# The FFN's last output tile made for 128 tokens at a time, with the update and the mixer's first product in halves

## The chip, the cores and the metric

The kernel runs on one core of one Trainium2 chip. The metric is the device time of one execution in microseconds (us); the median of the runs is compared. Engines are named as the profile names them: PE (TensorE, the matmuls), PEld (its weight loads), DVE (VectorE), ACT (ScalarE), POOL (GpSimd), SP (SyncE, which issues most transfers).

## What is computed

An encoder trunk of four layers on 256 tokens of width 1024, in float32. Each layer is a half-step feed-forward branch (FFN, SwiGLU, hidden width 2816), a token mixer, and a second FFN. Layers 0 and 3 use mixer A (chunked attention), layer 1 mixer B (a gated MLP with a mixing matrix over tokens), layer 2 mixer C (differential attention).

```python
def rms_norm(x, g):
    y = x * rsqrt(mean(x * x, axis=-1) + EPS)
    return y * g

def swiglu(h, w_in, w_out):
    gate, up = split(h @ w_in, 2, axis=-1)
    return (silu(gate) * up) @ w_out

for i in range(DEPTH):
    g = norm_g[i]
    x = x + 0.5 * rms_norm(swiglu(rms_norm(x, g[0]), ff1_w_in[i], ff1_w_out[i]), g[1])
    h = rms_norm(x, g[2])
    x = x + rms_norm(mixer(h), g[3])
    x = x + 0.5 * rms_norm(swiglu(rms_norm(x, g[4]), ff2_w_in[i], ff2_w_out[i]), g[5])
```

The norm after a branch needs the branch's whole output: the factor of a token is known only when all 1024 features of it are there. That is the junction this case is about.

## The kernel before

**Layout.** Activations are kept transposed: 128 features on the partitions, tokens along the free dimension, so `xr` (the residual stream) is 8 tiles of 128 features by 256 tokens. A weight is split on the chip into a high part in fp32r and the rest (`w_hi`, `w_lo`: a cast on ACT, L126, and a subtraction on DVE, L129), and so are the activations (`h` and `l`, stored side by side as `x[:, k, 0, :]` and `x[:, k, 1, :]`). A product is three passes: high by high, high by low, low by high.

**Weights.** `Stream` (`W`) loads raw pieces through SP into three raw buffers of two pieces each, splits them into eight slots, and hands them out with `peek` and `done`; `done(n, most)` frees n pieces and lets at most `most` new ones be split; `hold` stops splitting and `resume` starts it again. PE's, DVE's and ACT's instructions run in the order in which the program writes them.

**Forms of product.** `product2` (L175 to L186) makes one matmul of 512 columns (the weight's high part with the activations' high and low parts side by side) and one of 256 (the weight's low part). The two halves of the result are then added: ACT copies the second half (`share`), DVE adds. `product` (L164 to L171) makes three matmuls of 256 columns straight into one result, with no addition afterwards. `Wide` (L686 on) takes activations of 128 tokens as the weights and streams 512 columns of the weight matrix, for the mixers' first product; its result has tokens on the partitions, in two banks of PSUM, one for each half of the tokens.

**The FFN's end.** `ffn` (L557) makes eight output tiles d. Tiles 0 to 6 use `product2`; `Branch.joined` adds the halves, squares the tile, adds the square into `acc`, and scales the tile by the gain into `yg`. Tile 7 uses `product` (L168). Then `tile_done` sums the squares over the features with `column_sums` (matmuls with a column of ones, L243), `finish` makes the factor of each token (`inv_sqrt`: a square root on ACT, L251, a reciprocal on DVE, L253), `spread2` copies it to all partitions by matmuls (L258), and an `Update` is returned: x gains `yg` times the spread factor.

**Made ahead.** While this chain runs, PE has work that needs no factor: `Ahead`. Before a mixer (`wide=True`) it makes, for the first 128 tokens and k = 2 and 3, the mixer's first product of the old x and of `yg` apart (12 matmuls of 512 columns, L455); the second is scaled by the factor and added later (`scale`, `join`). Between a mixer and the second FFN, and between layers, it does the like for the FFN's first product (L457).

**The next stage's start.** `Normed` updates x in the order of `PARTS` (multiply on DVE, add on DVE, high part on ACT, low part on DVE), sums the squares of the new x, and PE follows through `Wide` in the order `JOIN` as the tiles get ready. After the last FFN there is no next stage: eight DVE passes over two tiles each (a multiply and an add, four times) and four transfers write the output.

Of the kernel before, what the change touches and what calls it, by code (L numbers as in the profile page):

```python
# [16 lines left out]
P = 128  # L17
# [33 lines left out]
YLATE = {4: (0, 1), 5: (2, 3)}  # L51
JOIN = _order([k for a, b in PARTS for k in range(a, b)])
# [4 lines left out]
def encoder_trunk_kernel(  # L57
# [207 lines left out]

    class Normed:


        def __init__(self, update, gain):
# [5 lines left out]
            if update is None:  # L275
                self.begin(gain)
            else:
# [39 lines left out]
        def high(self, gain, a, b):  # L317
            for k in range(a, b):
                nc.scalar.activation(self.h[:, k, :], xr[:, k, :], AF.Copy, scale=gain[:, k:k + 1])  # L319
# [12 lines left out]
        def low(self, gain, a, b):  # L332
            for k in range(a, b):
                nc.vector.scalar_tensor_tensor(
                    self.l[:, k, :], xr[:, k, :], gain[:, k:k + 1], self.h[:, k, :].bitcast(F32),
# [24 lines left out]
    class Branch:  # L360
# [37 lines left out]

        def finish(self):
# [7 lines left out]
    class Ahead:  # L407


        def __init__(self, gain, wide=False, late=False):  # L410
            self.gain, self.wide, self.late = gain, wide, late
            self.ks = (2, 3) if wide else (0, 1, 2, 3)
            self.x, self.y, self.todo = {}, {}, []
# [23 lines left out]
        def begin(self):  # L437

            self.ps, self.share = pair(), bank()
            for o, xs in ((self.ps[:, 0, :], self.x), (self.share, self.y)):  # L440
                for k in self.ks:
                    if self.wide:
                        wh, wl = [part.rearrange("p (k c) -> p k c", k=2)[:, k % 2, :] for part in W.peek(k // 2)]
                    else:
                        wh, wl = [part[:, k, :] for part in blocks(W.peek())]
# [5 lines left out]
        def __call__(self, n):  # L451
            while self.todo and n > 0:
                o, w_, x, first, last = self.todo.pop(0)
                if self.wide:
                    nc.tensor.matmul(o, x[:, 0:P], w_, start=first, stop=last, skip_group_check=True)  # L455
                else:
                    nc.tensor.matmul(o[:, 0:S], w_, x, start=first, stop=last, skip_group_check=True)  # L457
                n -= 2 if self.wide else 1

        def scale(self, update):  # L460

            if self.wide:
                self.fy = tmp.tile([P, 512], F32, tag="hf", bufs=3, name="fy")
                nc.scalar.activation(self.fy, self.share, AF.Copy, scale=update.f[:, 0:1])
            else:
                self.fy = tmp.tile([P, S], F32, tag="gs", name="fy")
                nc.scalar.copy(self.fy, self.share[:, 0:S])
                nc.vector.tensor_tensor(self.fy, self.fy, update.fb, op=ALU.mult)

        def join(self):  # L470
            o = self.ps[:, 0, :] if self.wide else self.ps[:, 0, 0:S]
            nc.vector.tensor_tensor(o, o, self.fy, op=ALU.add)

    class Update:


        def __init__(self, yg, f, fb, ahead):
            self.yg, self.f, self.fb, self.ahead, self.t = yg, f, fb, ahead, {}

        def multiply(self, a, b):  # L480
            t = tmp.tile([P, 2, S], F32, tag="upd", name="upd")[:, 0:b - a, :]
            nc.vector.tensor_tensor(
                t, self.yg[:, a:b, :], self.fb.unsqueeze(1).broadcast_to([P, b - a, S]), op=ALU.mult
# [3 lines left out]
        def add(self, a, b):  # L487
            nc.vector.tensor_tensor(xr[:, a:b, :], xr[:, a:b, :], self.t.pop(a), op=ALU.add)  # L488
# [68 lines left out]
    def ffn(l, which, update, ahead):  # L557
# [58 lines left out]
        nc.scalar.preload_act_table(AF.Sqrt)  # L616
        br = Branch(g_sb[:, l, 4 * which + 1, :], n, ahead)
        b = 0
        for d in range(KD):
# [22 lines left out]
            if ahead:  # L642
                ahead.x_parts(d)
        return br.finish()
# [41 lines left out]
    class Wide:  # L686


        def __init__(self, n):
            self.n, self.q, self.ahead = n, 0, n.ahead  # L690

        def block(self, piece, kk, low):
            wh, wl = [part.rearrange("p (k c) -> p k c", k=2)[:, kk % 2, :] for part in piece]
            for xs, ws in ((self.n.l, wh),) if low else ((self.n.h, wh), (self.n.h, wl)):
                for t in range(2):
                    if t == 0 and self.ahead and kk in self.ahead.ks:
                        continue
# [574 lines left out]
```

## Time and profile before

| | |
|---|---|
| median of 3 runs | 1940.93 us (1940.19 to 1941.04) |
| the profiled execution's own time | 1942.05 us |
| its span in the profile | 1940.3 us |
| mean granted TensorE clock | 0.999 |
| weight load (PEld) busy | 90% of the span |
| HBM traffic | 347.31 MB read, 1.05 MB written |

How to read the views: a row of the page or of the groups gives line, engine, operation, what is written and read, partitions x elements, count, then busy microseconds, mean nanoseconds of one, idle time ahead of it and what ended it. Successive matmuls overlap in the records, so the mean duration of one is not the distance from one to the next; that distance comes from the chain, which gives start, length and count. A row of the timeline begins with start and length in microseconds.

### The profile page before, as it was taken

To read this page: it belongs to the slowest core of one execution; us is meant where nothing else is said; L and a number is where in the kernel's file an instruction comes from. 1 tells how busy PE (TensorE), PEld (TensorE's weight loads), DVE (VectorE), ACT (ScalarE), POOL (GpSimd) and SP (SyncE) were. 2 spreads that over 40 slices of the span, in tenths; PEclk is the share of its full clock that TensorE was granted. 3 is DMA by queue.
4 is the path that set the end of the run, shared out by engine and by line. 5 is a ranking of instruction groups with operands and counts; after the bars stand their busy time and mean duration, and the time that the engine had idled before them with its cause. 6 is when DMAs were issued, how large, how long until landed. Compare 5 with 4: busy or idle time off the path is not lost.

```text
span 1940.3 us, 29924 instructions
## 1 busy us (share of the span) xinstructions
PE 1928.2 (99%) x12354; PEld 1741.4 (90%) x12354; DVE 1388.3 (72%) x1883; ACT 1168.6 (60%) x1797; POOL 5.2 (0%) x19
## 2 busy tenths in 40 slices
PE   9999999999999999999999999999999999999998
PEld 8888999888988899888988899988898889998887
DVE  6775767876777587876676668786768766868763
ACT  6655557656555566656565665775656555666552
POOL 0000000000000000000000000000000000000000
PEclk9999999999999999999999999999999999999999
DMA  7555524555455544655455544365445554535551
GB/s 257 203 193 197 194 109 152 218 194 195 154 207 183 203 168 151 229 186 198 147 213 188 188 158 169 109 214 196 177 163 205 194 197 168 196 115 186 200 201 44
DMA packets 50393, 350.30 MB, mean 181 GB/s; under 512 B 5712, under 2 KB 5968, under 8 KB 9040
## 3 DMA queue, kind: packets, MB, share of 16 engines
q1 hardware_dynamic: 48096, 341.86, 48.7%
q10 hardware_dynamic: 2160, 6.52, 0.9%
q8 instruction: 97, 1.59, 0.3%
q14 instruction: 40, 0.33, 0.0%
HBM read 347.31 MB, written 1.05 MB: 180 GB/s over the span
## 4 chain that ended last, share of the span: by engine, by line
PE 98%; DVE 1%; DMA 0%; ACT 0%; SPq 0%; issue 0%; DVEq 0%
PE pp_t L182 68%; PE pp_t L535 8%; PE pp_t L168 7%; PE pp_t L698 4%; PE pp_t L516 4%; PE pp_t L657 2%; PE pp_t L738 1%; PE pst_t L770 1%; PE pp_t L457 1%; PE pst_t L243 1%; PE pst_t L457 1%; PE pp_t L892 0%; PE pst_t L258 0%; DVE rbc L352 0%; PE pp_t L455 0%; DMA w_raw<-in_w 0%
## 5 line engine op out<-in xcount | busy, mean ns | idle before, releaser
L129 DVE TENSOR_TENSOR w_lo<-w_raw,w_hi 128x1024 fp32r<-128x1024 f32 (+1 forms) x649 | 775.7, 1218 | 61.8 <-ACT w_hi L126 61.6
L126 ACT CAST w_hi<-w_raw 128x1024 fp32r<-128x1024 f32 (+1 forms) x649 | 668.8, 1045 | 161.5 <-PE pp_t L182 130.1
L182 PE MATMUL pp_t<-xp,w_hi 128*128 128x512 f32 x2560 | 612.9, 391 | 0.0
L182 PEld LDWEIGHTS pp_t<-xp,w_hi 128*128 128x128 f32 x2560 | 470.2, 188 | 90.8
L182 PEld LDWEIGHTS pp_t<-xp,w_lo 128*128 128x128 f32 x2560 | 329.2, 191 | 16.1 <-DVE w_lo L129 3.4
L182 PE MATMUL pp_t<-xp,w_lo 128*128 128x256 f32 x2560 | 335.1, 283 | 2.6 <-DVE w_lo L129 2.6
L604 DVE TENSOR_TENSOR gu<-pp_t,share 128x512 f32<-128x512 f32 x160 | 110.4, 690 | 201.6 <-ACT share L603 201.6
L603 ACT COPY share<-pp_t 128x512 f32<-128x512 f32 x160 | 93.5, 584 | 145.9 <-PE pp_t L182 145.3
L182 PE MATMUL pp_t<-h,w_hi 128*128 128x512 f32 x672 | 169.0, 391 | 0.0
L576 ACT ACTIVATE gs<-gs 128x512 f32<-128x512 f32 x88 | 55.7, 633 | 145.5 <-DVE gs L575 145.5
L182 PE MATMUL pp_t<-l,w_hi 128*128 128x512 f32 x560 | 142.6, 391 | 0.0
L182 PEld LDWEIGHTS pp_t<-h,w_hi 128*128 128x128 f32 x672 | 122.1, 189 | 22.6
L535 PE MATMUL pp_t<-xp,w_hi 128*128 128x256 f32 x832 | 125.0, 289 | 1.1 <-ACT w_hi L126 0.7
L182 PEld LDWEIGHTS pp_t<-l,w_hi 128*128 128x128 f32 x560 | 102.6, 188 | 21.1 <-DVE l L585 1.6
L535 PEld LDWEIGHTS pp_t<-xp,w_hi 128*128 128x128 f32 x832 | 112.2, 194 | 3.5 <-ACT w_hi L126 1.2
L373 DVE TENSOR_TENSOR yg<-pp_t,share 128x256 f32<-128x256 f32 x56 | 23.8, 425 | 108.8 <-ACT share L372 108.8
L182 PEld LDWEIGHTS pp_t<-h,w_lo 128*128 128x128 f32 x672 | 91.1, 191 | 5.0
L182 PE MATMUL pp_t<-h,w_lo 128*128 128x256 f32 x672 | 95.2, 282 | 0.0
L182 PE MATMUL pp_t<-l,w_lo 128*128 128x256 f32 x560 | 80.6, 283 | 0.0
L319 ACT ACTIVATE xp<-xr,g_sb 128x256 fp32r<-128x256 f32 x96 | 44.8, 504 | 55.9 <-DVE xr L488 54.0
L182 PEld LDWEIGHTS pp_t<-l,w_lo 128*128 128x128 f32 x560 | 75.4, 191 | 2.8
L535 PE MATMUL pp_t<-xp,w_lo 128*128 128x256 f32 x416 | 74.3, 285 | 0.0
(201 smaller groups left out, 2254.3 us busy)
## 6 DMA issues: line engine op xcount, KB each, us to landing
w_raw<-in_w SPq DMA_DIRECT2D x322, 1024.0 KB, 4.8
l<-in_a_bias ACTq DMA_DIRECT2D x8, 512.0 KB, 7.5
w_raw<-in_w SPq DMA_DIRECT2D x3, 512.0 KB, 8.6
out_y<-xr SPq DMA_DIRECT2D x4, 256.0 KB, 2.1
xr<-in_x_t SPq DMA_DIRECT2D x2, 384.0 KB, 6.8
w_raw<-in_w SPq DMA_DIRECT2D x2, 256.0 KB, 5.0
l<-in_b_ws ACTq DMA_DIRECT2D x1, 512.0 KB, 5.8
l<-in_b_ln_g ACTq DMA_DIRECT2D x1, 512.0 KB, 7.3
```

The costliest lines, as they stand in the source:

```text
L126: nc.scalar.copy(hi[:, cols], raw[:, cols])
L129: nc.vector.tensor_tensor(lo[:, cols], raw[:, cols], hi[:, cols].bitcast(F32), op=ALU.subtract)
L168: nc.tensor.matmul(o, w_[:, at + i, :], x(k)[:, low, :], start=(start and i == 0 and m == 0), stop=(stop and k == ks[-1] and m == 2),)
L182: nc.tensor.matmul(o[:, 0:S] if low else o, (wl if low else wh)[:, at + i, :], x(k)[:, 0, :] if low else x(k), start=(start and i == 0 and ...
L319: nc.scalar.activation(self.h[:, k, :], xr[:, k, :], AF.Copy, scale=gain[:, k:k + 1])
L457: nc.tensor.matmul(o[:, 0:S], w_, x, start=first, stop=last, skip_group_check=True)
L516: nc.tensor.matmul(o, part[:, k, :], n.x[:, k, int(low), :], start=((k, low) == JOIN[0] and i == 2 and part is ws[i][0]), stop=((k, low) = ...
L535: nc.tensor.matmul(o, part[:, k, :], n.x[:, k, low, :], start=(at == 0), stop=(at == 3 * KD - 1))
L576: nc.scalar.activation(gs, gs, AF.Silu)
L603: nc.scalar.copy(share, ps[:, :, S:2 * S])
L604: nc.vector.tensor_tensor(at.t[:, e], ps[:, :, 0:S], share, op=ALU.add)
L698: nc.tensor.matmul(self.ps[:, t, :], xs[:, kk, t * P:(t + 1) * P], ws, start=((kk, low) == self.order[0] and ws is wh and not (t == 0 and ...
```

## The change

It affects five of the eight FFNs: the first of each layer, which stands ahead of a mixer, and the very last (`halved = which == 0 or not ahead`).

- Tile 7 of these FFNs is made by `last_halves`: for each half t of the tokens, 22 matmuls of 256 columns (high and low parts of 128 tokens side by side) and 22 of 128 columns. The sum, the squares, the factor and its spread are made for each half. Those of half 0 run while PE works on half 1. The three weight pieces of the tile are given back only after both halves, behind `hold`.
- `Normed.halves` takes the place of the update in `PARTS` order. It updates 128 tokens of the tiles in the order of `HALF_PARTS`, lets `Wide` make the first half of the mixer's product (24 matmuls of 512 columns), with the steps of half 1's factor laid in between, and then updates the other 128 tokens. `Wide.first` makes the second half.
- `Ahead(wide=True)` is removed with all its cases, so nothing is made ahead of a mixer. The `Ahead` of the other junctions stays.
- At the end of the kernel the output's half 0 is updated and written first, in two transfers, then half 1.

```diff
+HALF_PARTS = ((0, 1), (1, 2), (2, 4), (4, 6), (6, 8))
...
+        def halves(self, up, gain):
+            self.wide = Wide(self)
+            br = up.br
+            for a, b in HALF_PARTS:
+                if a == 6:
+                    br.half_sum(1)
+                up.multiply(a, b, 0)
+                up.add(a, b, 0)
+                self.high(gain, a, b, 0)
+            br.half_square(1, lambda: self.low(gain, 0, 4, 0))
+            self.wide.half(0, 0, 17)
+            br.half_factor(1, lambda: self.low(gain, 4, 6, 0))
+            self.low(gain, 6, KD, 0)
+            self.wide.half(0, 17, 20)
+            br.half_spread(1)
+            self.wide.half(0, 20, 24)
+            for a, b in HALF_PARTS:
+                up.multiply(a, b, 1)
+                up.add(a, b, 1)
+                self.high(gain, a, b, 1)
+            self.low(gain, 0, KD, 1)
+            W.resume(1)
+            W.settle()
+            for a in (0, 2, 4, 6):
+                self.square(a)
+            self.total()
+            W.pump(1)
...
+        def last_halves(self, blocks):
+            self.o = pair()
+            self.fs, self.fbs = {}, {}
+            for t in range(2):
+                todo = []
+                cols = tokens(t)
+                for run in blocks:
+                    turn[0] = not turn[0]
+                    for low in (False, True) if turn[0] else (True, False):
+                        todo += [(low, wl if low else wh, x) for wh, wl, x in run]
+                for i, (low, w_, x) in enumerate(todo):
+                    nc.tensor.matmul(
+                        self.o[:, t, 0:P] if low else self.o[:, t, 0:2 * P], w_, x[:, 0, cols] if low else x[:, :, cols],
+                        start=(i == 0), stop=(i == len(todo) - 1), skip_group_check=True,
+                    )
+                    if t == 1 and i == 19:
+                        self.half_factor(0)
+                    if t == 1 and i == 29:
+                        self.half_spread(0)
+                if t == 0:
+                    self.half_sum(0)
+                    self.half_square(0)
+            return Update(self.yg, None, None, None, self)
+
+        def half_sum(self, t):
+            share = tmp.tile([P, 2, S], F32, tag="upd", name="share")[:, 0, 0:P]
+            nc.scalar.copy(share, self.o[:, t, P:2 * P])
+            nc.vector.tensor_tensor(self.yg[:, KD - 1, tokens(t)], self.o[:, t, 0:P], share, op=ALU.add)
+
+        def half_square(self, t, then=lambda: None):
+            y, acc = self.yg[:, KD - 1, tokens(t)], self.acc[:, tokens(t)]
+            sq = tmp.tile([P, S], F32, tag="sq1", name="sq1")[:, 0:P]
+            nc.scalar.activation(sq, y, AF.Square)
+            nc.scalar.activation(y, y, AF.Copy, scale=self.gain[:, KD - 1:KD])
+            then()
+            nc.vector.tensor_tensor(acc, acc, sq, op=ALU.add)
+
+        def half_factor(self, t, then=lambda: None):
+            ss = bank()[:, 0:1]
+            nc.tensor.matmul(ss, self.acc[:, tokens(t)], ones[:, 0:1], start=True, stop=True)
+            then()
+            self.fs[t] = inv_sqrt(ss, eps2_t if self.n else eps_t, 1, 1.0 / D)
+
+        def half_spread(self, t):
+            self.fbs[t] = bank()[:, 0:P]
+            spread(self.fs[t], self.fbs[t])
...
+            up = br.last_halves(runs)
+            W.hold()
+            W.done(i)
+            return up
...
+        def half(self, t, a, b):
+            for i in range(a, b):
+                k, low, m = self.todo[i]
+                nc.tensor.matmul(
+                    self.ps[:, t, :], self.n.x[:, k, low, tokens(t)],
+                    W.peek(k // 2)[m].rearrange("p (k c) -> p k c", k=2)[:, k % 2, :],
+                    start=(i == 0), stop=(i == len(self.todo) - 1), skip_group_check=True,
+                )
+
+        def first(self):
+            self.half(1, 0, len(self.todo))
+            W.done(4, 3)
...
-        update = ffn(l, 0, update, Ahead(g_sb[:, l, 2, :], True))
+        update = ffn(l, 0, update, None)
...
+    fill = Warm()
+    fill(6)
+    update.multiply(0, 4, 0)
+    result(0, 4, 0)
+    update.multiply(4, KD, 0)
+    br.half_sum(1)
+    br.half_square(1, lambda: result(4, KD, 0))
+    br.half_factor(1)
+    fill(4)
+    br.half_spread(1)
+    for a, b in ((0, 4), (4, KD)):
+        update.multiply(a, b, 1)
+        result(a, b, 1)
```

`result(a, b, half)` adds the update to x for these tiles and tokens and issues the transfer of them. The order `todo` of `Wide` is: for each k the high activations with the weight's high and low part, then for each k the low activations with the high part.

More of the change, by code (lines that the diff above doesn't have):

```diff
@@ L276, in __init__ @@
                 self.begin(gain)
+            elif update.halved:
+                self.halves(update, gain)
             else:
@@ L453, in __call__ @@
                 o, w_, x, first, last = self.todo.pop(0)
[L454 to L458, printed above, removed]
-        def scale(self, update):
[L462 to L468, printed above, removed]
+                nc.tensor.matmul(o[:, 0:S], w_, x, start=first, stop=last, skip_group_check=True)
@@ L470, in join, with __init__ @@
+                n -= 1
+        def scale(self, update):
+            self.fy = tmp.tile([P, S], F32, tag="gs", name="fy")
+            nc.scalar.copy(self.fy, self.share[:, 0:S])
+            nc.vector.tensor_tensor(self.fy, self.fy, update.fb, op=ALU.mult)
         def join(self):
-            o = self.ps[:, 0, :] if self.wide else self.ps[:, 0, 0:S]
+            o = self.ps[:, 0, 0:S]
             nc.vector.tensor_tensor(o, o, self.fy, op=ALU.add)
     class Update:
-        def __init__(self, yg, f, fb, ahead):
+        def __init__(self, yg, f, fb, ahead, halved=None):
@@ L616, in ffn @@
         nc.scalar.preload_act_table(AF.Sqrt)
+        halved = which == 0 or not ahead
         br = Branch(g_sb[:, l, 4 * which + 1, :], n, ahead)
         b = 0
-        for d in range(KD):
+        for d in range(KD - 1 if halved else KD):
             apart = d < KD - 1
@@ L643, in ffn @@
                 ahead.x_parts(d)
+        if halved:
+            runs, k, i = [], 0, 0
+            while k < NJ:
+                wh, wl = blocks(W.peek(i))
+                n_ = min(KD - b, NJ - k)
+                runs.append([(wh[:, b + m, :], wl[:, b + m, :], hidden(k + m)[:, 0]) for m in range(n_)])
+                k, b, i = k + n_, 0, i + 1
+            up = br.last_halves(runs)
+            W.hold()
+            W.done(i)
+            return up
         return br.finish()
@@ L695, in block @@
                 for t in range(2):
-                    if t == 0 and self.ahead and kk in self.ahead.ks:
-                        continue
                     nc.tensor.matmul(
                         self.ps[:, t, :], xs[:, kk, t * P:(t + 1) * P], ws,
-                        start=((kk, low) == self.order[0] and ws is wh and not (t == 0 and self.ahead)),
+                        start=((kk, low) == self.order[0] and ws is wh),
                         stop=((kk, low) == self.order[-1]), skip_group_check=True,
@@ L710, in run @@
                     soon()
-                if low and kk % 2 and not self.ahead:
+                if low and kk % 2:
                     if kk == KD - 1:
@@ L716, in run @@
                     self.q = (kk + 1) // 2 % 4
-            if self.ahead:
-                self.ahead.join()
-                W.done(4, most)
-            self.ahead = None
     BLOCKS = ((0, 0), (1, 1), (1, 0))
@@ L773, in attention @@
     def attention(n, softmax, transposes, v_done, mix, prepare=lambda: None, soon=lambda: None):
-        wide = Wide(n)
-        wide.run()
+        wide = n.wide
+        wide.first()
         ps_v = wide.ps
@@ L948, in v_done @@
                 nc.vector.bn_stats(st[:, t, c, :], v[:, t, c * 512:(c + 1) * 512])
-        wide = Wide(n)
-        wide.run()
+        wide = n.wide
+        wide.first()
         for k in range(KD):
```

56 lines of the change are left out of this document (31 added, 25 removed).

## The prediction

> **What bounds the kernel now.** I read the page first (busy shares, then the chain that ended last), then the chain in order of time around the first place the change touches, then the same chain at the other places, then the groups by shape for durations, and last the vector engines' groups. PE is TensorE, DVE VectorE, ACT ScalarE.
>
> ```profile
> span 1940.3 us, 29924 instructions
> PE 1928.2 (99%) x12354; PEld 1741.4 (90%) x12354; DVE 1388.3 (72%) x1883; ACT 1168.6 (60%) x1797; POOL 5.2 (0%) x19
> PE 98%; DVE 1%; DMA 0%; ACT 0%; SPq 0%; issue 0%; DVEq 0%
> 188.52 7.92 PE pp_t L168 x66
> 196.44 0.34 PE pst_t L243 x4
> ...
> 200.70 9.63 PE pp_t L698 x42
> 210.33 2.87 PE pp_t L535 x24
> 213.21 0.34 PE pst_t L243 x4
> 213.55 2.98 PE pp_t L535 x24
> 216.52 0.44 PE pst_t L258 x4
> ```
>
> PE carries 98% of the chain: a microsecond on PE's own list is a microsecond of time, one on DVE or ACT counts only where PE stands still for it. The chain rows are columns of start, length, what. They show the first site (layer 0, FFN 1 into mixer A): the last output tile is 66 matmuls in 7.92 us, so **120 ns** for one of 256 columns; then 4.26 us of sums, spreads and the 12 matmuls made ahead; then 42 matmuls of 512 columns in 9.63 us, **229 ns** each. From the tile's start to the mixer's next product: 210.33 - 188.52 = **21.81 us**. The other three sites, and the tail:
>
> ```profile
> 678.71 7.92 PE pp_t L168 x66
> 690.83 13.24 PE pp_t L698 x58
> 1130.69 7.92 PE pp_t L168 x66
> 1152.48 2.87 PE pp_t L535 x24
> 1619.48 7.92 PE pp_t L168 x66
> 1641.26 2.87 PE pp_t L535 x24
> 1921.78 7.90 PE pp_t L168 x66
> 1932.06 1.28 DVE upd L482 x2
> 1935.99 0.60 DVE xr L488
> 1936.59 0.60 DVEq L1267
> ```
>
> Layer 2 and 3: 21.79 and 21.78. Layer 1: at 13.24/58 = 0.228 each the first 42 end at 700.41, so 21.70. In the tail the tile's first matmul is at about 1921.6 and the last add ends at 1937.19: **15.57 us**, the only stretch where DVE is the chain. The span ends 3.1 us later; the out_y transfers cover that.
>
> **The change, part by part.**
>
> *1. The tile in halves.* 66 matmuls of 256 columns become 88: 44 of 256 (120 ns) and 44 of 128. The columns streamed are the same, 22 x 768; the weight loads rise from 66 to 88. No fp32r matmul of 128 columns is in this trace. The nearest rows:
>
> ```profile
> L994 PE MATMUL pp_t<-l,l 128*128 128x128 f32 x32 | 4.3, 277 | 0.0
> 729.58 0.89 PE pp_t L994 x8
> L738 PE MATMUL pp_t<-qk 64*128 64x128 f32 x288 | 19.3, 280 | 0.0
> 225.60 1.54 PE pp_t L738 x24
> L994 PEld LDWEIGHTS pp_t<-l,l 128*128 128x128 f32 x32 | 3.9, 192 | 0.2 <-issue 0.2
> L893 PEld LDWEIGHTS pp_t<-h,l 128*64 128x64 f32 x56 | 4.7, 137 | 1.3
> ```
>
> With full 128x128 f32 weights, 128 columns take 0.89/8 = **111 ns**; with 64 rows, where two matmuls can lie side by side, 1.54/24 = **64 ns**. And the column sums, of one single column, still take 0.34/4 = 85 ns. So the time does not fall with the columns here; I take the load of the weights as the floor. A load of 128 columns lasts 192 ns and one of 64 lasts 137: 55 ns per 64 columns, some 110 for 128, which fits. Low end 64 ns, high end 222 (an f32 matmul is recorded as two instructions, 2 x 111, if the narrow product loses fp32r's rate). I take 111, the row with the same weights. The tile: 44 x (0.120 + 0.111) = 10.16 us against 7.92, **+2.24**.
>
> [...]
>
> *2. PE's other work per site.* Removed: 12 matmuls of 512 made ahead, of which only 6 saved a Wide matmul, and the waits around them. Added: Wide is whole, 48 x 0.228 = 10.94; two column sums and two spreads of 2 records each, 0.11 each, 0.88. PE's own sum: 10.16 + 0.88 + 10.94 = **21.98 against 21.81**. So nothing is won on PE even if it never waits.
>
> *3. Where PE waits.* The durations of half-width vector work:
>
> ```profile
> L482 DVE TENSOR_TENSOR upd<-yg,pst_t 128x512 f32<-128x512 f32 x37 | 25.1, 679 | 0.9 <-PE pst_t L258 0.8
> L482 DVE TENSOR_TENSOR upd<-yg,pst_t 128x256 f32<-128x256 f32 x22 | 9.2, 417 | 9.0 <-PE pst_t L258 9.0
> L1089 DVE SCALAR_TENSOR_TENSOR ex<-ex,rl 128x128 f32<-128x128 f32 x8 | 2.8, 352 | 0.0
> L319 ACT ACTIVATE xp<-xr,g_sb 128x256 fp32r<-128x256 f32 x96 | 44.8, 504 | 55.9 <-DVE xr L488 54.0 <-DMA g_sb<-in_gains 1.6 <-DMA xr<-in_x_t 0.2
> L755 ACT ACTIVATE ex<-s,nm 128x128 f32<-128x128 f32 x48 | 19.0, 396 | 41.9 <-DVE nm L747 24.3 <-DVE nm L750 17.5
> L372 ACT COPY share<-pp_t 128x256 f32<-128x256 f32 x56 | 20.8, 371 | 41.3 <-PE pp_t L182 41.3
> L251 ACT ACTIVATE sd<-pst_t,eps_t 128x2 f32<-128x2 f32 x16 | 4.2, 260 | 4.2 <-PE pst_t L243 4.2
> L253 DVE RECIPROCAL rs<-sd 128x2 f32<-128x2 f32 x17 | 2.8, 165 | 26.2 <-ACT sd L251 26.2
> 197.85 0.17 DVE L253 RECIPROCAL rs<-sd 128x2 f32<-128x2 f32 x1 [2.07 <-ACT sd L251]
> 198.88 0.42 DVE L482 TENSOR_TENSOR upd<-yg,pst_t 128x256 f32<-128x256 f32 x1 [0.87 <-PE pst_t L258]
> 199.34 0.42 DVE L488 TENSOR_TENSOR xr<-xr,upd 128x256 f32<-128x256 f32 x1
> ```
>
> DVE: 679 for 512 and 417 for 256 is 0.15 us fixed plus 1.02 ns a column, so about 0.29 for 128, 0.33 for the low part (352 in a like row). ACT: 396 for 128 in a like row, so 0.40 for a high part, two in a row 0.30 apart; a share copy 0.26. Halving a tile halves the data, not the fixed parts. A dependent DVE pair starts 0.46 apart at 256 columns (198.88, 199.34), so 0.04 lies between. I lay the queues out by these, with 0 at the tile's first matmul:
>
> - Half 0 of the tile ends at 5.1; share, add, square and sum of it are done by 6.6, before the factor's place (7.4, after 20 matmuls) and the spread's (8.8). PE waits for none. The first update starts at 9.2, the first high part is ready at 10.25, the tile ends at 10.6. Covered.
> - Then the update of half 0 stops at `half_sum(1)`, put ahead of tiles 6 and 7 in DVE's and ACT's order. ACT reaches its share copy only at 12.6, behind the high parts of tiles 4 and 5; DVE, idle from 12.0, adds at 12.9; tile 6's high part ends at 14.4. PE wants it at 13.6: **1.0 us** of waiting, after 0.2 for tile 2.
> - The sum of half 1 is ready at 15.3, its spread runs at 16.7 on PE (0.1 waited). The update of half 1 starts at 17.1 and its first high part ends at 18.2; PE is through with half 0 at 17.85: **0.5**. After that PE follows the chain of multiply, add and high part: 0.1 and 0.35 more until tile 3.
>
> That is 2.26 us of waits. 21.98 + 2.26 = 24.24, **+2.43 a site**. In the old order the same row of updates ran under 12 matmuls and 42; the new one has less cover and more fixed parts.
>
> *4. Weights.*
>
> ```profile
> L126 ACT CAST w_hi<-w_raw 128x1024 fp32r<-128x1024 f32 x647 | 667.5, 1047 | 159.3 <-PE pp_t L182 130.1 <-PE pp_t L168 13.4 <-DMA w_raw<-in_w 11.3
> L129 DVE TENSOR_TENSOR w_lo<-w_raw,w_hi 128x1024 fp32r<-128x1024 f32 x647 | 774.3, 1219 | 59.5 <-ACT w_hi L126 59.3
> ```
>
> Two weight pieces that were split while the tile ran (ACT 1.05, DVE 1.22 each) now wait for `hold` to end, and Wide's `done(4, 3)` puts three of them ahead of `sums` on ACT. By the same layout ACT takes its square root at 29.9 and DVE the reciprocal at 30.4, and mixer A's token spread, wanted at 30.4 on PE, comes at 30.75: **+0.3** where the four bias transfers are issued from ACT too (two sites). In C and B I take 0: fewer issues in C, a later spread in B. In the old order the wait was nil, the spread following its 24 matmuls at 213.55 + 2.98 = 216.53. If ACT were late by 1 us more this would be +1 a site. The transfers queue behind the held pieces, but three raw buffers hold six pieces; I cost that at nothing, with PE at some 3 us a piece as cover.
>
> *5. Work removed from DVE and ACT* while the tiles 0 to 6 run (parts made ahead): off the chain, nothing.
>
> *6. The tail.* Same layout: tile ends at 10.6 on PE (was 7.9), half 0 is updated under it, half 1's add at 11.4, its sum at 12.2, spread at 13.8, then four DVE passes of 512 columns instead of eight: last add at 16.56 against 15.57, **+1.0**. The output goes in pieces of 512 bytes instead of 2 KB a row; nothing for it, at most 1.
>
> **Sum**: 4 x 2.43 + 2 x 0.3 + 1.0 = **+11.3 us**. The profiled execution took 1942.05 (span 1940.3 and 1.75 around it), so 1953.4 there; it stands 1.1 above the median of 1940.93, so **1952.3**.
>
> **Rivals.**
> (a) *Narrow matmuls are paced by their columns, 64 ns, and the waits stay.* For: L738. Against: L994, the single-column sums. The tile is then 8.1; by the same layout a site is +0.7 (in A +1.0), because the vector chain sets the pace in PE's place; the tail -0.75. Sum +2.6, 1943.5.
> (b) **Faster**: *the weight loads hide behind the stream, at the tile's 44 narrow matmuls, and the update keeps ahead of PE.* Price on PE alone: 8.1 + 0.88 + 10.94 = 19.92, -1.9 a site; tail -0.75; sum -8.3, 1932.6. It decides from the point where the waits stay below 1.1 us a site; I count over 2.
> (c) *fp32r's rate is lost below 256 columns*, 222 ns: +6.5 a site (+6.85 in A), tail +5.8, sum +32.6, 1973.5. Against: the records of 111 belong to plain f32.
> (d) *The halves don't run apart*: half 1's matmuls wait until half 0 of the pair is read. The add ends 0.8 after half 0 does; with 0.14 to restart, 0.9 x 5 = +4.7 on top, 1957. Nothing in the trace shows two banks of one pair read and written at once.
>
> **How the numbers follow.** Forecast 0.63; (a) 0.15; (b) 0.12; (c) 0.05; (d) 0.05. 0.2% is 3.9 us, about what a measurement of this kernel can tell from no change. Faster 0.12, same 0.15, slower 0.73. The likeliest case alone, with 100 to 120 ns and the waits a microsecond a site either way, is 1946 to 1959. From 1941 to 1961 the range holds forecast, (a) and (d), 0.83.
>
> **What would show it.** Right: groups of 128-column matmuls near 111 ns apart; a tile of some 10.2 us; PE gaps ended by ACT's high part of tile 6, then of tiles 0 and 2 in half 1; tile start to mixer product about 24.2; last add 16.6 after its tile began. Wrong: narrow matmuls at 64 or less, or a Wide product without gaps (then the durations of half-width work or the order of the queues were misread), or the token spread in A late by more than 0.5.

## The result, and the profile after

The changed kernel takes 1964.84 us (median of 4 runs, 1963.09 to 1967.45) against 1940.72 for the kernel before: 1.0124 times as long, 95% interval 1.0111 to 1.0136. The direction was forecast; the time, 1952.3 with a range up to 1961, was not.

First the page of the changed kernel: span, busy time of each engine, and its shares of the chain of work that ended last.

```profile
span 1961.4 us, 30157 instructions
PE 1935.8 (99%) x12410; PEld 1744.1 (89%) x12410; DVE 1392.7 (71%) x1960; ACT 1173.5 (60%) x1834; POOL 5.2 (0%) x19
PE 91%; DVE 5%; DMA 2%; ACT 2%; issue 1%; ACTq 0%; SPq 0%; DVEq 0%
```

PE's share of the chain was 98% and is 91%: the chain now leaves PE for DVE, ACT and DMA. The list of waits, over the whole kernel and for PE alone (waiting line, releaser, us in total, times, longest), names the three large ones. The list of the kernel before has no counterpart to any of them.

```profile
PE pp_t L842 <- DVE qk L832: 5.4, 3, 2.9
PE pp_t L791 <- ACT xp L356: 3.5, 8, 0.7
PE pp_t L449 <- DVE yg L465: 3.4, 5, 0.7
```

L791 is `Wide` waiting for the high parts, as forecast. L449 is the tile in halves itself, waiting for its own sum, a rival with a chance of 0.05. L842 is the mixers' scores, 17 us behind the end of the changed stretch, and stood in no part of the forecast. All three are seen in the chain around the first site (start, length, what):

```profile
186.61 5.10 PE pp_t L449 x44
...
191.74 0.27 ACT share L464
...
192.03 0.30 DVE yg L465
...
192.38 2.50 PE pp_t L449 x20
...
201.34 0.41 ACT xp L356
...
201.79 1.42 PE pp_t L791 x5
...
216.24 8.03 DMA w_raw<-in_w
...
224.29 1.06 ACT w_hi L128
...
226.52 1.03 DVE w_lo L131
...
227.66 1.23 DVE qk L832
...
229.02 2.19 PE pp_t L842 x24
```

44 matmuls take 5.10 us, as forecast (44 x 0.231/2 = 5.08). Then PE stops: half 1's first matmul starts at 192.38, after half 0's share copy on ACT and its add on DVE, though it writes another bank. At 201.79 `Wide` goes on behind the high part of tile 6. The rows from 216.24 on are the third wait: a raw weight piece that took 8.03 us to land, its cast on ACT, the low part of it on DVE, behind that DVE's scaling of the first query and key, and only then the scores.

**Where the +21 lie.** The profiled executions took 1942.05 and 1963.09. I cut both by PE's records: "site" is from the tile's first matmul to the first matmul of the mixer's query and key product, "mixer" from there to the first matmul of `product` in its output projection, which makes tiles 4 to 7 of it (L170; in the kernel before L168). B has no such first product, so both stand together there.

| | before | after | difference | forecast |
|---|---|---|---|---|
| sites A layer 0, C, A layer 3 | 21.81, 21.79, 21.78 | 25.11, 25.12, 25.11 | +9.96 | +7.29 |
| B with its site | 71.93 | 75.68 | +3.75 | +2.43 |
| mixer A, layer 0 | 88.33 | 91.94 | +3.61 | +0.3 |
| mixer C | 86.87 | 87.44 | +0.57 | 0 |
| mixer A, layer 3 | 88.33 | 91.26 | +2.93 | +0.3 |
| tail, first matmul to last add | 15.57 | 17.39 | +1.82 | +1.0 |
| last add to the span's end | 3.1 | 3.4 | +0.3 | 0 |
| span's start to the first site | 188.36 | 186.45 | -1.9 | 0 |

That is +21.0. The last row is no effect of the change: with the same code ahead of the first site the other changed kernels start it between 186.3 and 188.4, and the kernel of experiment 12, whose code up to there is that of the kernel before, at 186.28. The medians differ by 3.1 more because the profiled run of the changed kernel is its fastest, 1.75 below its median, and that of the kernel before lies 1.3 above its own.

**What a late score costs.** Mixer A of layer 0 loses 3.61 us, but PE waits only 2.03 there. The windows of the changed kernel, 1 us each (columns: window, its length, busy time and instructions of PE, PEld, DVE, ACT and POOL, granted clock, DMA share, GB/s), show the rest:

```profile
228.00:229.00 1.00, 0.00 (x0) 0.01 (x1) 1.00 (x2) 1.00 (x2) 0.00 (x0) 1.00 1.06 270
229.00:230.00 1.00, 0.98 (x16) 1.00 (x18) 1.00 (x1) 0.56 (x1) 0.00 (x0) 0.93 0.53 205
230.00:231.00 1.00, 1.00 (x12) 0.91 (x9) 0.94 (x4) 0.00 (x0) 0.00 (x0) 0.50 0.99 418
231.00:232.00 1.00, 1.00 (x6) 0.86 (x5) 1.00 (x4) 0.49 (x2) 0.00 (x0) 0.50 0.94 385
232.00:233.00 1.00, 1.00 (x6) 1.00 (x6) 1.00 (x1) 0.97 (x5) 0.00 (x0) 0.50 0.00 0
233.00:234.00 1.00, 1.00 (x10) 1.00 (x9) 1.00 (x4) 1.00 (x4) 0.00 (x0) 0.86 0.00 0
```

PE is busy again from 229.02, but from 229.9 to 233.3 at half its clock; the 24 score matmuls take 2.19 us instead of 1.54. The shortfall summed over these rows is 0.07 + 0.5 + 0.5 + 0.5 + 0.14 = **1.71 us**, and 2.03 + 1.71 = 3.74 against 3.61. The same wait in layer 3 is longer, 2.88, and no clock was lost; the mixer lost 2.93. So a late score costs its wait and, at times, a stretch of half clock.

Which of the two it is goes with where the wait falls. In the changed kernel's trace the half clock lasts 3.41 us, from 229.87 to 233.28. In the trace of experiment 10 the clock drops to half at 229.54 and at 1673.38, which is 1443.84 us apart or 423 times 3.4133. So it is elsewhere: of the ten traces that show the clock over the first 1958 us (the kernels before and after, and experiments 1, 2, 3, 5, 7, 8, 10 and 12) eight have more than one such drop, and in each of these all drops lie on a grid of 3.413 us. I summed, in each cell of the grid at full clock, the time in which PE had no matmul. Leaving out the first 15 us of the kernel, where at most 1.08 us (experiment 7, ahead of 10.72) was followed by half clock, a cell with some 2 us or more was followed by half clock every time, and one with 1.76 us or less never, in these ten traces. In the changed kernel the cell from 226.46 to 229.87 holds the whole wait of 2.03. In layer 3 a cell ends at 1673.71, inside the wait of 2.88, and leaves 1.12 us of it on one side and 1.76 on the other. The shortfall of 1.71 is one cell at half clock, half of 3.413, and 2.03 us without a matmul in the cell ahead of it were enough.

**Why the score is late.** Windows of 8 us around the first site, the kernel before first, then the changed one; the last column is GB/s:

```profile
188.50:196.50 8.00, 8.00 (x70) 8.00 (x68) 4.43 (x5) 3.70 (x7) 0.00 (x0) 1.00 0.57 216
196.50:204.50 8.00, 8.00 (x40) 6.40 (x40) 5.65 (x13) 3.39 (x9) 0.00 (x0) 1.00 0.06 27
204.50:212.50 8.00, 8.00 (x46) 7.02 (x45) 7.39 (x13) 5.57 (x11) 0.00 (x0) 1.00 0.26 84
212.50:220.50 8.00, 8.00 (x69) 8.00 (x69) 5.23 (x7) 7.97 (x11) 0.64 (x3) 1.00 0.98 379
```

```profile
186.60:194.60 8.00, 7.32 (x64) 7.12 (x63) 1.44 (x4) 2.58 (x7) 0.00 (x0) 1.00 0.27 113
194.60:202.60 8.00, 7.33 (x47) 6.08 (x47) 6.14 (x19) 3.83 (x12) 0.00 (x0) 1.00 0.00 0
202.60:210.60 8.00, 7.73 (x34) 5.56 (x33) 7.12 (x24) 5.11 (x13) 0.00 (x0) 1.00 0.00 0
210.60:218.60 8.00, 8.00 (x65) 7.80 (x65) 7.71 (x10) 6.85 (x10) 0.00 (x0) 1.00 0.75 264
218.60:226.60 8.00, 8.00 (x69) 8.00 (x69) 3.59 (x4) 5.14 (x7) 0.93 (x4) 1.00 1.02 422
```

Before, weights land until the tile's end and again in the window that begins at 204.5. Now nothing moves for two whole windows, and then the weights and the 2 MB of position bias for mixer A fall on each other at 422 GB/s with the DMA engines full. The late start comes from SP's queue: the raw buffers come free when DVE has made the low part of what lies in them, and the tile's weight pieces are given back only after both halves. The longest such wait of SP around the first site, from 184 to 232 us, changed kernel first (last column):

```profile
SPq L105 <- DVE w_lo L131: 42.4, 6, 26.3
```

```profile
SPq L103 <- DVE w_lo L129: 36.1, 6, 15.9
```

26.3 us in place of 15.9.

The kernel before has such a meeting as well: its window from 212.5 shows 379 GB/s with the DMA engines nearly full. Of the transfers that SP issues from the tile's first matmul on, the first that the bias slows down is the third there (at 215.58) and the second now (at 216.24). Their rows among the DMA issues (last column: us to landing), the kernel before first:

```profile
w_raw<-in_w SPq DMA_DIRECT2D x1, 1024.0 KB, 8.7
```

```profile
w_raw<-in_w SPq DMA_DIRECT2D x1, 1024.0 KB, 8.0
```

Before, the 8.7 us cost nothing, and DVE's timeline says why (start, length; the kernel before, then the changed one):

```profile
222.76 1.22 DVE L728 TENSOR_TENSOR qk<-pp_t,rbc 128x1024 f32<-128x1024 f32 x1 [0.42 <-PE pp_t L535]
225.44 1.22 DVE L129 TENSOR_TENSOR w_lo<-w_raw,w_hi 128x1024 fp32r<-128x1024 f32 x1 [1.45 <-ACT w_hi L126]
```

```profile
225.38 2.36 DVE L131 TENSOR_TENSOR w_lo<-w_raw,w_hi 128x1024 fp32r<-128x1024 f32 x2 [2.46 <-ACT w_hi L128]
227.66 1.22 DVE L832 TENSOR_TENSOR qk<-pp_t,rbc 128x1024 f32<-128x1024 f32 x1
```

Before, the scale of query and key waits for PE alone, and the low parts of the late transfer come behind it. With two splits put off by `hold`, the transfer that meets the bias is one whose low parts stand ahead of the scale. So the wait in mixer A needs both: the splits put off, and the slow transfer.

### The profile page after: what moved, and what is told of

Read it like the earlier page. It is cut to its first block, busy times and chain, and to the rows that moved or that the text cites. A ratio compares the mean times of both kernels' runs of the same rounds, so it can differ in the third digit from the quotient of the medians.

```text
span 1961.4 us, 30157 instructions
## 1 busy us (share of the span) xinstructions
PE 1935.8 (99%) x12410; PEld 1744.1 (89%) x12410; DVE 1392.7 (71%) x1960; ACT 1173.5 (60%) x1834; POOL 5.2 (0%) x19
## 4 chain that ended last, share of the span: by engine, by line
PE 91%; DVE 5%; DMA 2%; ACT 2%; issue 1%; ACTq 0%; SPq 0%; DVEq 0%
PE pp_t L184 67%; PE pp_t L616 6%; PE pp_t L597 4%; PE pp_t L170 4%; PE pp_t L750 2%; PE pp_t L449 2%; PE pp_t L806 2%; DVE w_lo L131 1%; DMA w_raw<-in_w 1%; PE pp_t L842 1%; DVE xr L569 1%; DVE upd L562 1%; PE pst_t L874 1%; ACT w_hi L128 1%; PE pp_t L537 1%
## 5 line engine op out<-in xcount | busy, mean ns | idle before, releaser
L356 ACT ACTIVATE xp<-xr,g_sb 128x256 fp32r<-128x256 f32 (+1 forms) x128 | 52.9, 450 | 60.4 <-DVE xr L569 55.6
```

What stands on the lines that cost most here:

```text
L356: nc.scalar.activation(self.h[:, k, cols], xr[:, k, cols], AF.Copy, scale=gain[:, k:k + 1])
```

## The experiments

The theories: **(H)** the halves of the tile wait for each other because both lie in one pair; **(W)** the given-back weights come too late, the raw transfers meet the bias transfers, and the scores wait behind the late low parts; against W the rivals that the splits of three pieces at once are simply in front of the scores (**S**), or that the attention lost time for a reason of its own. The matmul's floor was tried as well. Medians are of 4 runs unless said, and what a mixer loses is counted from the kernel before.

### 1. Two pairs instead of one

```diff
-            self.o = pair()
+            self.o = [pair(), pair()]
...
-                        self.o[:, t, 0:P] if low else self.o[:, t, 0:2 * P], w_, x[:, 0, cols] if low else x[:, :, cols],
+                        self.o[t][:, 0, 0:P] if low else self.o[t][:, 0, 0:2 * P], w_, x[:, 0, cols] if low else x[:, :, cols],
```

> The changed kernel (1964.84 median, 1963.1 profiled) with one edit: the two halves of tile 7 are written into two PSUM pairs instead of the two banks of one. Theory 'one pair': the gap in the tile between the last matmul of half 0 and the first of half 1 (0.85 us, ended by DVE's add of half 0) comes from the pair being one tile in the order of reads and writes, not from the data. Then half 1 starts 0.12 us after half 0's last, each of the five places is 0.75 to 0.9 us shorter, sum -4 to -4.5: about 1960.5. Rival 'the sum itself': half 1 waits for the add for another reason (the same wait stays, 1964.8). The waiting on late weights in mixer A (3.6 us in layer 0, 3.0 in layer 3) stays by both.

Measured 1960.9 (one of the four runs took 4902.98 us, which no trace explains; the other three 1960.39 to 1961.08), ratio of these three 1.0104 (1.0087 to 1.0121). Sites 24.18, 24.18, 24.19; tail 16.50. The chain has the gap no longer, 64 matmuls in one row:

```profile
188.16 7.33 PE pp_t L449 x64
```

H holds: 0.93 less at a site and 0.89 in the tail. B's site by itself, to the first matmul of `Wide.run`, went from 25.13 to 24.18, so 4.6 in all; the later part of B lost 0.6 of it again (51.15 after 50.55), and the medians differ by 3.9. What is left of the site, 24.18, and of the tail, 16.50, is the forecast's own sum (24.24 and 16.56). The mixers still lose: +2.15 and +4.54. The second is the same wait with the half clock on it. This row (PE's timeline: start, length, then in brackets the wait and its releaser) is layer 3's first scores:

```profile
1672.38 2.93 PE L842 MATMUL pp_t<-qk 64*128 64x128 f32 x24 [2.90 <-DVE qk L832]
```

In windows of 0.2 us the clock is at 0.50 from 1672.4 to 1675.8: 2.90 + 1.71 = 4.61. The changed kernel had its 1.71 in layer 0, where this one has none behind a wait of 2.08.

### 2. One weight piece given back inside the tile

```diff
+                    if t == 1 and i == 2 * len(blocks[0]) - 1:
+                        W.done()
+                        W.settle()
                     if t == 1 and i == 19:
...
             W.hold()
-            W.done(i)
+            W.done(i - 1)
```

> The changed kernel with one edit: the tile's first weight piece is given back after its last use in half 1, and its successor split at once, instead of all three behind the hold. Theory 'late request': a raw buffer comes free some 16 us earlier, so 1 MB of weights is transferred in the 21 us in which the DMA engines stand idle, and no longer collides with mixer A's 2 MB of bias transfers. Then mixer A from its first product on takes what it took before: layer 0 -3.6, layer 3 -3.0, mixers B and C -0.5 each, sum -7: about 1957.5, and the spread between runs (1963.1 to 1967.5) shrinks to under 1 us. The split costs the update of half 0 up to 0.5 us a site (+2), if DVE's low part lands ahead of the first multiply. Rival 'vector queue': the scale of q and k is late because three splits stand ahead of it on ACT and DVE, whatever the transfers do; then the time stays within 1 us of 1964.8 and the scores of the first heads still wait 2 us.

Measured 1959.89, ratio 1.0101 (1.0086 to 1.0116): 5.0 less where 7 were expected, and the runs still spread over 3.6 us (1958.77 to 1962.41) where under 1 was expected. In the list of PE's waits the scores now stand with

```profile
PE pp_t L845 <- DVE qk L835: 1.6, 2, 1.2
```

instead of 5.4 in three, and no half clock is left behind the scores. Mixer A loses 0.78 and 1.25, mixer C nothing. In the DMA view 1 MB now lands in the stretch that was empty. W holds for most of the loss, with ACT's bias issues where they were; it leaves 2 us.

### 3. Both

```diff
-            self.o = pair()
+            self.o = [pair(), pair()]
...
+                        W.done()
+                        W.settle()
```

> Two PSUM pairs for the halves and the first weight piece given back early, together. Apart they gave -3.9 and -5.0. If they are independent, the sum: 1956.0. If the earlier end of the tile only lets PE arrive earlier at a transfer that is no sooner there, less: 1958 to 1960.

Measured 1956.09 (1955.56 to 1960.5), ratio 1.0082 (1.0066 to 1.0099). By the medians the two gains add up. Piece by piece they do not quite: the sites take 24.5 where two pairs alone gave 24.18, and mixers A lose 0.76 and 1.66, so a part of the agreement is luck.

### 4. A second piece given back

```diff
+                    if t == 1 and i == 2 * len(blocks[0] + blocks[1]) - 1:
+                        W.done()
...
-            W.hold()
-            W.done(i - 1)
+            W.held = True
+            W.done(i - 2)
```

> Two PSUM pairs, and two of the tile's three weight pieces given back as half 1 is through with them: the splits inside the tile are then those of the kernel before. Theory: what is left of the lateness in the mixers (1.1 in layer 0, 1.3 in layer 1, 2.0 in layer 3 with one piece given back) goes, -3.5; the second split's cast stands ahead of the first high part on ACT and costs up to 0.4 a site, +1.6. So 1954 (1953 to 1955.5), near the prediction's own sum of 1952.3. Rival 'one piece was enough, the rest is of another kind': 1956 to 1958.

Measured 1956.94, ratio 1.0085 (1.0069 to 1.0102): a miss, no gain. Mixers A lose 1.63 and 1.11, and C loses 0.73 again where one piece given back left it whole. Giving back more is not better without end; why it lost in C was not followed up.

### 5. Mixer A without the bias transfers

The position bias is set to zero and not loaded, so the transfers and their four issues on ACT are gone; the learned position bias is left out of the result.

```diff
-            nc.scalar.dma_start(b, a_bias[i, :, a:a + 4])
+            nc.gpsimd.memset(b, 0.0)
```

> The changed kernel without mixer A's bias: POOL fills its tiles with zeros and the four transfers of 512 KB in each of the two mixers A are left out (so the learned position bias is missing from the scores). Theory 'collision': what costs mixer A 3.6 and 3.0 us over the kernel before, and mixer C, which has the same deferred splits and 128 KB of its own, only 0.6, is that the weights requested late share the DMA engines with 2 MB of bias. Then both mixers A fall to C's excess: layer 0 -3, layer 3 -2.4, about 1959.5, and the runs lie closer together. Rival 'deferred splits': the two splits put off (ACT 1.05 and DVE 1.22 us each) stand ahead of the scale whatever the transfers do; then 1964 to 1965.

Measured 1958.66, ratio 1.0094 (1.0079 to 1.0109). Mixers A are back at 88.33 and 88.32 us, to the hundredth what they took before the change, and the chain goes from the product to the scores on PE alone:

```profile
219.46 8.64 PE pp_t L616 x72
228.10 1.54 PE pp_t L842 x24
```

The weights are given back as late as in the changed kernel, and the low parts stand ahead of the scale as they did, but now without a gap among them (DVE's timeline):

```profile
221.09 4.63 DVE L131 TENSOR_TENSOR w_lo<-w_raw,w_hi 128x1024 fp32r<-128x1024 f32 x4 [1.50 <-ACT w_hi L128]
225.64 1.22 DVE L832 TENSOR_TENSOR qk<-pp_t,rbc 128x1024 f32<-128x1024 f32 x1
```

The scale ends at 226.86, 1.24 us before PE comes to the scores at 228.10, and nothing is lost in mixer A. That takes away S as a cause by itself there: the splits in front hurt when their transfer is slow. Mixer C, which has no such bias, keeps its 0.6 (87.47); its transfer in the same place lands in 4.7 us, and its scores wait 0.50, so there the splits in front cost that much by themselves.

### 6. Without the bias, with two pairs

```diff
-            self.o = pair()
+            self.o = [pair(), pair()]
...
-            nc.scalar.dma_start(b, a_bias[i, :, a:a + 4])
+            nc.gpsimd.memset(b, 0.0)
```

> Two PSUM pairs, and mixer A's bias transfers left out (zeros instead, so the position bias is missing). If those two are what the prediction missed, its own sum is left: four sites at 2.4 each, C's 0.6, the tail 0.9 and its longer output 0.3, B's 0.5 to 1.5: about 1952.5 (1951.5 to 1954). If more is in it: above 1955.

Measured 1953.05 (1953.02 to 1954.4), ratio 1.0065 (1.0048 to 1.0081). With both unforeseen losses out, the time is that of the forecast's sum, 1952.3, within a microsecond. A part of this is luck: the 0.3 forecast for each mixer A was not spent, while the later part of B lost 1.5, C 0.6 and the output 0.3 that were forecast as nothing. The learned bias is not read here, so this is a test of the sum and no version to use.

### 7. The bias from POOL's queue

```diff
-            nc.scalar.dma_start(b, a_bias[i, :, a:a + 4])
+            nc.gpsimd.dma_start(b, a_bias[i, :, a:a + 4])
```

> The changed kernel with mixer A's four bias transfers issued by POOL instead of ACT; the same 2 MB at about the same time. Leaving them out also took four issues of some 0.4 us each off ACT. Theory 'collision of transfers': the lateness stays, 1963 to 1967. Rival 'the issues on ACT': mixers A fall to 88.3 us as without the bias, about 1958.5.

Measured 1957.45, ratio 1.0087 (1.0072 to 1.0102); mixers A again 88.33 and 88.32. That is the time of the rival. POOL's timeline says why it tells less than was meant:

```profile
199.72 1.73 POOL L956 DMA_DIRECT2D l<-in_a_bias  x3 [198.34 <-DVE upd L562]
```

On ACT the issues stand behind the square sums. In the changed kernel's timeline of ACT the first is this:

```profile
211.87 0.82 ACTq L956 DMA_DIRECT2D l<-in_a_bias  x2
```

POOL has nothing of its own ahead of them and issues as soon as a step of DVE's update releases it. Counted from the tile's first matmul the first issue comes at 11.6 us instead of 25.4, in the empty stretch. So the transfers no longer meet the weights and ACT's issues are gone, both at once; the run is a cure (-7.4 us with the bias in place). What divides the two is the transfer itself, the one that stands ahead of the scale. Counted in the same way it is issued at 29.80 in the changed kernel and at 29.73 both in experiment 5 and here, so ACT's issues put the request off by 0.07 us only. But it lands 4.8 us after it, in experiment 5 and here alike,

```profile
w_raw<-in_w SPq DMA_DIRECT2D x1, 1024.0 KB, 4.8
```

and not 8.0. The 3.27 us by which it lands earlier (34.56 instead of 37.83 in experiment 5) are the wait of 2.03 and the 1.24 that the scale then has in hand. In layer 3 the transfer takes 8.80 us, lands 4.19 later than in experiment 5, and PE waits 2.88. The meeting of the transfers is what mixer A waits for, and next to nothing of the wait is left for the issues on ACT.

### 8. Fewer splits ahead of the first scores

S tried as a cure: one piece split there instead of three.

```diff
-            W.done(4, 3)
+            W.done(4, most)
...
-        wide.first()
+        wide.first(1)
...
-        project_pair(n, False, early, scaled(0))
+        project_pair(n, False, early, scaled(0), 1)
```

> The changed kernel with fewer splits let through at the start of an attention mixer (one instead of three behind Wide's first product, one instead of two a piece in the first q and k product); the weights are requested from the same raw buffers. Theory 'a split in front': PE never lacks weights; the scale of q and k is late because DVE and ACT stand at the split of a piece that PE needs only some 15 us later and whose transfer is late. With the splits behind the scale instead of ahead of it the scores don't wait: layer 0 -3.6, layer 3 -3.0, about 1958.3, and less spread. Rival 'PE lacks weights': with fewer splits PE runs dry in the q and k products, the wait turns up at the matmuls of the next pieces, and the time is 1965 or more.

Measured 1969.99, ratio 1.015 (1.0134 to 1.0165): 5 us worse. The first scores are in time, but the splits come back in front of the second ones. The chain of this kernel, further on in mixer A of layer 0:

```profile
239.94 0.98 DVE w_lo L131
...
241.08 2.35 DVE w_lo L131 x2
243.44 1.14 DVE qk L832
...
244.62 1.61 PE pp_t L842 x24
```

Three low parts stand ahead of the second scale there. In mixer C the second scores wait 3.73 us, and the half clock follows from 1199.0 to 1202.4, 1.71 more; C takes 4.8 longer than in the changed kernel, and B 1.0, while the mixers A, at 90.92 and 90.93, take a little less.

### 9. The same with two pairs and one piece given back

```diff
-            self.o = pair()
+            self.o = [pair(), pair()]
...
+                        W.done()
+                        W.settle()
...
-            W.done(4, 3)
+            W.done(4, most)
```

> Two pairs, the piece given back early, and the splits behind the scale, together. If the pair and the late weights are the whole of what the prediction missed, what is left is its own sum: tile 7 with 88 matmuls +2.24 and PE's waits on the vector chain 2.26 a site, 2.43 net a site, the tail +1.3: 1952.3 (1951 to 1954). If something else is in it, it stays above 1955.

Measured 1966.58, ratio 1.0132 (1.0117 to 1.0147), far from the 1952.3 expected and 10.5 above experiment 3: putting the splits off costs more still where the weights are in time.

### 10. The sum of half 1 later

`half_sum(1)` after the update of half 0, for the forecast's longest wait in `Wide`.

```diff
-                if a == 6:
-                    br.half_sum(1)
...
+            br.half_sum(1)
             br.half_square(1, lambda: self.low(gain, 0, 4, 0))
```

> The changed kernel with one edit: the sum of half 1 comes after the update of all eight tiles of half 0 instead of ahead of tiles 6 and 7. By the queue layout of the prediction PE's wait of 0.9 to 1.0 us for tile 6's high part goes, but half 1's factor comes later and PE waits for it instead: -0.37 a site, -1.5 in all, about 1963.3 (the weight lateness moves this by 1 or 2). Rival 'the order costs its whole wait': -0.95 a site, -3.8, about 1961.

Measured 1964.45, ratio 1.0121 (1.0106 to 1.0136), no different from the changed kernel. The sites take 24.77, 24.82 and 24.78: 0.33 less each, the size that the layout of the queues gave. The time does not show it; in the profiled run mixer A of layer 3 loses 5.7 us. Its first scores:

```profile
1674.17 2.94 PE L841 MATMUL pp_t<-qk 64*128 64x128 f32 x24 [2.92 <-DVE qk L831]
```

The wait is 2.92, as in the others; the clock is then at half for twice as long, from 1673.4 to 1680.2, a shortfall of 3.41: a cell of the grid ends inside the wait with 2.13 us of it, the other 0.79 lie in the next cell, at half clock, and the clock stays at half for one more. In the changed kernel, in that with two pairs and in this one the waits at these two places are 2.03 to 2.92, and the shortfall behind them was 0 twice, 1.71 three times and 3.41 once, in no order of the waits; whether there was any is in each case as the grid has it.

### 11. Twice the columns in the narrow matmuls

Each matmul of 128 columns streams them twice, into two places.

```diff
-                        self.o[:, t, 0:P] if low else self.o[:, t, 0:2 * P], w_, x[:, 0, cols] if low else x[:, :, cols],
+                        twice if low else self.o[:, t, 0:2 * P], w_,
+                        x[:, 0:1, cols].broadcast_to([P, 2, P]) if low else x[:, :, cols],
```

> The changed kernel with each of the 128-column matmuls of tile 7 made 256 columns wide (the same 128 columns twice, the second time into an unused part of the bank); the count of weight loads stays at 88. Theory 'the load is the floor': 128 columns take 112 ns, 256 take 120; 44 x 8 ns = +0.35 us a place, +1.8 over five places, about 1966.5. Rival 'the columns': twice the columns are 44 x 53 ns = +2.3 a place, +12, 1976.

Measured 1967.5, ratio 1.0136 (1.0121 to 1.0151). The half tile of 44 matmuls takes 5.29 us in the chain instead of 5.10:

```profile
187.16 5.29 PE pp_t L450 x44
```

22 matmuls with twice the columns cost 0.19 us, 9 ns each. So 128 columns are not paced by their columns but by something that 256 columns have to pay too, 111 against 120 ns. The weight load, one for each, is what both share; in PE's records the loads of the narrow matmuls start 111 to 113 ns apart, and so do the column sums of one single column with full weights in the kernel before, once the first has started (196.306, 196.418, 196.530).

### 12. The end of the kernel alone

The tile in halves only in the last FFN, everything ahead of it as before: the kernel before with the change's lines for the tile and the output, under this condition.

```diff
+        halved = not ahead
```

> The kernel before with the end alone changed: only the last FFN's tile 7 and the output go by halves, the junctions ahead of the mixers keep the old order and the work made ahead. The changed kernel's tail took 17.4 us from the tile's first matmul to the last add against 15.57, and 0.3 more until the span ends: +2.1, about 1942.8. Rival 'the tail wins what it is meant to, and the loss lies with the mixers alone': 1938 to 1940. The layers ahead of it must be as in the kernel before to 0.3 us.

Measured 1943.11 (10 runs, 1942.05 to 1944.02) against 1940.78, ratio 1.0011 (1.0002 to 1.0021). Sites and mixers are those of before, the tail takes 17.38, as in the changed kernel. The end loses by itself, 1.8 to the last add and some 0.3 behind it.

No kernel here beats the one before. The best with the whole computation is experiment 3, 15 us behind. Two pairs, one piece given back and the bias from POOL together were not run; by the forecast's own sum some 1952 would be the best to expect of them.

## Why the prediction was wrong, point by point

- **The tile** (part 1): right. 44 matmuls in 5.10 us, and 111 ns for 128 columns with the load as the floor; (a) and (c) are out, and the faster rival (b) with (a)'s price. One row was misread on the way, without harm: the column sums are not 85 ns apart but 112, since the 0.34 us hold a first distance of 0.03, and this speaks for the floor even more.
- **PE's other work, and where PE waits** (parts 2 and 3): right. With two pairs a site is 24.18, forecast 24.24. Its waits are 24.18 - 21.98 = 2.20, forecast 2.26. One by one, read from the distances between the starts of `Wide`'s matmuls, they are 0.19 for tile 2, 0.94 for tile 6, and 0.49 and 0.34 in half 1, where 0.2, 1.0, 0.5 and 0.35 were laid out; and the term of the late sum, tried by itself, had its size. This is the mechanism and no luck.
- **The halves run side by side**: wrong. Rival (d) is what happens, with its own price: 0.93 a place and 4.6 in all, forecast 0.9 and 4.7. The mistake was its chance of 0.05. The forecast noted that nothing in the trace showed two banks of one pair read and written at once, and then took the reading that suited the sum. The queue layout was right for two tiles, and the program has one.
- **Weights** (part 4): wrong, and the larger part. The step that failed is "The transfers queue behind the held pieces, but three raw buffers hold six pieces; I cost that at nothing, with PE at some 3 us a piece as cover." It looked at whether PE has weights, and PE never lacked them here. It laid the splits put off out as far as the token spread, and did not follow the late transfers to what they meet (the bias) nor the late low parts to what queues behind them on DVE (the scale for the scores). That cost 2.03 and 2.88 us of waiting in the mixers A, 0.50 in C, and the half clock behind one of them; the three mixers lost 7.1 where 0.6 was forecast. The 0.3 a mixer that it did name, for the token spread, is not seen: PE's timeline of the changed kernel has no wait there (that of experiment 3 has one, of 0.53).
- **B**: 3.75 where 2.43 was forecast. 3.4 of it are the site, 21.7 before and 25.13 now, with 0.93 for the halves. The later part of B lost 0.4 here, and from nothing (experiment 2) to 1.6 (experiment 5) in the other kernels; where it lost 0.9 or more, PE waits 0.6 us for DVE's `us` in B's output projection, some 63 us after the tile's first matmul. Why DVE is late there no run set apart, and it stays open.
- **The tail** (part 6): 16.50 with two pairs, forecast 16.56; with one pair the halves add 0.9. The output in short rows, taken at nothing, cost 0.3.

The sum 4 x 2.43 + 1.0 stood on terms that the runs bear out (experiment 6). What was missing came from two places outside PE's own list: an order between halves, and a queue a mixer away.

## What to carry to other kernels

When a change holds weights back longer, the question is not only whether the next product has its weights: follow the transfers to those they will now meet, and the splits to what stands behind them on the same engine. The transfer of 8.7 us in the kernel before cost nothing, because what needed it stood behind the urgent work in its engine's order. Two halves in two banks of one tile did not overlap here, and in two tiles they did, for 0.93 us a site; two banks of one tile are no evidence of an overlap. And where a median moves by steps, look at the granted clock behind each wait before reading the median as the size of an edit.

## What the runs showed of the hardware

A wait of PE of 2.0 to 2.9 us cost up to 3.41 us more in half clock after PE was busy again, in steps of 1.71, and sometimes nothing (the changed kernel, experiments 1 and 10); in mixer C a wait of 3.73 cost 1.71 (experiment 8). Where the wait falls on the grid of 3.413 us fits the steps: past the first 15 us, some 2 us or more without a matmul in one cell at full clock (2.03 in the changed kernel) were followed by half clock each time in the ten traces, 1.76 or less never. Why the clock stayed at half for a second cell in experiment 10 is open. The runs of the changed kernel scatter over 4.4 us and those of the kernel before over 0.9. Their granted clocks fit: 0.998 for 1963.09 and 1963.59, 0.997 for 1966.09 and 0.996 for 1967.45, and 0.002 of 1965 us are 3.9 us; only one run of each was profiled. And an fp32r matmul with 128 x 128 weights costs nearly the same at 128 columns as at 256, 111 against 120 ns, so that splitting tokens in two does not halve the narrow matmul's time.
